# Later mixing of v, a new spread of conv taps, and output weights split in other steps, in a hybrid encoder layer on one core

## Chip, cores and metric

The kernel runs on 1 core of one Trainium2 chip. The metric is the time of the device for one execution, in microseconds (us). Five engines work side by side, each with its own queue of instructions: TensorE (PE, matmuls and transposes), VectorE (DVE), ScalarE (ACT), GpSimd (POOL) and SyncE (SP), which here issues every DMA.

## The reference

One layer of an encoder: x of 2048 tokens by 1024 is normalised, multiplied by one input matrix, and the columns go to three mixers, each with a gate. Their outputs are concatenated, multiplied by an output matrix, added to the normalised x and normalised again. Cut to what is computed:

```python
x = layer_norm(x, ln_in_g, ln_in_b)
h = einsum('bsd,de->bse', x, w_in)
au, av, ag, ba, bb, bg, cq, ck, cv, cg = split(h, ...)   # 256 x6, 512, 128, 128, 512
# A: spatial gating in chunks of 128 tokens, 4 heads of 64
v  = layer_norm(gelu(av), ln_g, ln_b)
v  = einsum('hij,bcjhd->bcihd', w_spatial, v) + b_spatial
ya = gelu(au) * v * silu(ag)
# B: depthwise convolution, 31 taps over the tokens, 256 channels
y  = conv(ba * sigmoid(bb), conv_w) + conv_b
yb = silu(layer_norm(y, g, b)) * silu(bg)
# C: attention over +-128 tokens, 8 query heads, 2 key/value heads, sink and bias
yc = attention(cq, ck, cv, sink, bias) * silu(cg)
y  = concatenate([ya, yb, yc]) @ w_out
out = layer_norm(2 ** 0.25 * x + y, post_ln_g, post_ln_b)
```

All arrays are float32.

## The kernel before

**Products.** Every product of the large matrices is made from two parts, a rounded `hi` and the rest `lo`: `hi*hi + hi*lo + lo*hi`, three matmuls. The normalised x lies transposed in four tiles `xc0` to `xc3` of 512 tokens, hi and lo. `feat(w, c, ...)` makes one tile `ft_n_c` of 128 columns by 512 tokens in 24 matmuls of 128x512 (lines 139 to 141). The weights of a column block come as `raw_f`, are rounded by ACT to `hi_f` and subtracted to `lo_f`.

**Stages.** First the layer norm of x, the columns av (written to DRAM as `gv_d`), keys and values. Then 72 steps in the list `steps`, each one `feat` and its evacuation: steps 0 to 15 the conv's bb and ba (n = 0 to 3), 16 to 31 the pairs au and ag (n = 4 to 7), 32 to 47 the queries (n = 8 to 11, evacuated to `qh_d` and `ql_d`), 48 to 55 cg (gates of the attention, silu, to `g_d`), 56 to 63 bg, and from `tail0` = 64 on the pairs (16, c), (17, c), that is the rest of cg, mixed with slots of the attention (`SLOTS`). Behind the steps the attention and the output projection run block by block of 128 tokens to the end.

**Work hung on the steps.** `hooks` holds functions for a step. `vln_tile(t)` loads a tile `gw` of gelu(av), normalises it on DVE (with two small operations on GpSimd, `nse` and `nsr`) and writes it hi and lo into `vacc`, `vglu` or, for the last four, `vshi`/`vslo`. `spatial(g)` mixes four such tiles: four tiles `sp` of PSUM (pool tag psE, two buffers, which `ft` tiles of odd steps use too), whose sum with the bias ACT copies to `so`, to be stored. `turn_spatial` transposes the spatial weights `wsr` through `ps_wt`; `prep_conv` loads and transposes the conv weights `cwr` through `ps_cw`. `cwr` and the `gw` tiles share the tag "cn" with two buffers. `conv_step(n)` emits n of the conv's 62 operations on DVE into `acc0`, then `acc1` (line 399); a sum `taps` decides how many a step gets, the last two come in step 47. From `cl0` = 48 on `conv_ln_tile` transposes `acc` to tiles `cl`, normalises them, and `conv_back` turns them back. `split_wo(k, hf)` loads a piece `wor` of the output weights, makes `woh` (ACT) and `wol` (DVE) and stores both; its buffers (tags ug, shi, slo, two each) are those of the evacuations' hi and lo.

**Tail.** `open_f32` and `open_f32r` open arenas in the place of `xc0` and `xc1`, `open_wo(0)` loads the first half of the split output weights, `wo0`, into the place of `xc2`, `open_wo(1)` into that of `xc3`. `start_block(i)` loads q of block i in two DMAs (`qh_d`, `ql_d`) and casts it; `scores` makes `s{i}_{h}` and `ptrans` the transposes `pt`; `oproj` multiplies into `out{i}_{hf}`.

**What sets the order.** A scheduler sorts each engine's instructions by its own estimate of when they are ready; the order in the code is only its input. So an edit in the first steps can move instructions of the last ones. SP issues its DMAs strictly in its order, so one that waits for data or for a buffer holds all behind it; in the trace a DMA also waits for the one eight issues ahead of it (that of `gw` at 144.67 us for `wsr`).

Of the kernel before, what the change touches and what calls it, by code (L numbers as in the profile page):

```python
# [55 lines left out]
def trunk_kernel(  # L56
# [77 lines left out]
    def feat(w, c, name, o=0, n=CH, tag="psD"):  # L134
        ps = psp.tile([P, n], F32, tag=tag, name="ft_" + name)
        hi, lo = w
        for k in range(NK):
            xh, xl = xc[c][:, 0, k, o:o + n], xc[c][:, 1, k, o:o + n]
            T.matmul(ps, hi[:, k, :], xh, start=(k == 0), stop=False)  # L139
            T.matmul(ps, hi[:, k, :], xl, start=False, stop=False)  # L140
            T.matmul(ps, lo[:, k, :], xh, start=False, stop=(k == NK - 1))  # L141
        return ps
# [159 lines left out]
    def want(n):  # L302
        if n < len(plan) and n not in wts:
            wts[n] = prep_w(plan[n][0], f"f{n}", V if 4 <= n < 14 else G)
# [12 lines left out]
    def prep_conv():  # L317
        cwr = pm.tile([KW, 256], F32, tag="cn", name="cwr")
        SY.dma_start(cwr, conv_w[0])
        for j, src in enumerate((conv_b, conv_ln_g, conv_ln_b)):  # L320
            SY.dma_start(cpar[:, j, :], src[0].rearrange("(a p) -> p a", p=P))
        ps = psp.tile([P, 2, KW + 1], F32, tag="psE", name="ps_cw")
        for a in range(2):
            T.transpose(ps[:, a, 0:KW], cwr[:, a * P:(a + 1) * P], ident[0:KW, 0:KW])
        V.tensor_copy(cw[:, :, 0:KW], ps[:, :, 0:KW])
# [11 lines left out]
    def prep_spatial():  # L337
        wsr = pm.tile([P, 4, P], F32, tag="tmp", name="wsr")
        SY.dma_start(wsr, w_spatial[0].rearrange("h i j -> i h j"))
        SY.dma_start(bsp, b_spatial[0].rearrange("h i -> i h"))  # L340
        SY.dma_start(vgb[:, 0, :], gmlp_ln_g[0].partition_broadcast(P))
        SY.dma_start(vgb[:, 1, :], gmlp_ln_b[0].partition_broadcast(P))
        return wsr

    def turn_spatial(wsr):
        ps = psp.tile([P, 4 * P], F32, tag="psE", name="ps_wt")
        for h in range(4):
            T.transpose(ps[:, h * P:(h + 1) * P], wsr[:, h, :], ident)
        S.copy(wth, ps)
        V.tensor_tensor(out=wtl, in0=ps, in1=f32(wth), op=ALU.subtract)  # L350
# [19 lines left out]
    def spatial(g):  # L370

        so = [pm.tile([P, 2, 256], F32, tag="tmp", name=f"so{g}_{j}") for j in range(2)]
        for h in range(4):
            ps = psp.tile([P, TPC, HD], F32, tag="psE", name=f"sp{g}_{h}")
            fs = slice(h * HD, (h + 1) * HD)
            cs = slice(h * P, (h + 1) * P)
            if g < 3:
                parts = [(ps, varena[g % 2][:, 0, :, fs], varena[g % 2][:, 1, :, fs])]
            else:
                parts = [(ps[:, 2 * j:2 * j + 2, :], vsp[j][0][:, :, fs], vsp[j][1][:, :, fs]) for j in range(2)]  # L380
            for o, vh, vl in parts:
                T.matmul(o, wth[:, cs], vh, start=True, stop=False)
                T.matmul(o, wth[:, cs], vl, start=False, stop=False)
                T.matmul(o, wtl[:, cs], vh, start=False, stop=True)
            for j in range(2):
                S.activation(so[j][:, :, fs], ps[:, 2 * j:2 * j + 2, :], AF.Identity, bias=bsp[:, h:h + 1])
        for j in range(2):
            r0 = (g * TPC + 2 * j) * P
            SY.dma_start(spo_d[r0:r0 + 2 * P, :].rearrange("(c p) f -> p c f", p=P), so[j])
# [17 lines left out]
    def conv_step(n):  # L407
        for _ in range(n):
            if avail[0] <= 0:
                return  # L410
            avail[0] -= 1
            next(conv)
# [42 lines left out]
    def load_mixed(a, c):  # L455
        sp = pm.tile([P, TPC, P], F32, tag="ug", name=f"spo{a}_{c}")
        SY.dma_start(sp, spo_d[c * CH:(c + 1) * CH, a * P:(a + 1) * P].rearrange("(b p) f -> p b f", p=P))
        spo[a, c] = sp

    def mixed(a, c):  # L460
        sp = spo.pop((a, c))
        pt = psp.tile([P, CH], F32, tag="psA", name=f"spT{a}_{c}")
        for j in range(TPC):
            T.transpose(pt[:, j * P:(j + 1) * P], sp[:, j, :], ident)
        spt[a, c] = pt
        u = a * NC + c + 1
        if u < 2 * NC:
            load_mixed(u // NC, u % NC)

    def evac(kind, a, c, ps):  # L470
        cs = slice(c * CH, (c + 1) * CH)
        ps_cs = slice(PAD + c * CH, PAD + (c + 1) * CH)
        if kind == "bb":
            if c == 0:
                g_ = pm.tile([P, SEQ + 2 * PAD + 2], F32, tag="glu", name=f"glu{a}")
                V.memset(g_[:, 0:PAD], 0.0)
                V.memset(g_[:, PAD + SEQ:SEQ + 2 * PAD], 0.0)
                glu.append(g_)
            S.activation(glu[a][:, ps_cs], ps, AF.Sigmoid)
        elif kind == "ba":  # L480
            last[0] = V.tensor_tensor(out=glu[a][:, ps_cs], in0=ps, in1=glu[a][:, ps_cs], op=ALU.mult).ins
            if c == NC - 1:
                avail[0] += KW
        elif kind == "au":
            tm = pm.tile([P, CH], F32, tag="tmp", name=f"gu{a}_{c}")
            S.activation(tm, ps, AF.Gelu_apprx_tanh)
            pt = spt.pop((a, c))
            last[0] = V.tensor_tensor(out=tm, in0=pt, in1=tm, op=ALU.mult).ins
            ug[a, c] = tm
        elif kind == "cq":  # L490
            fs = slice(a * P, (a + 1) * P)
            split_store(ps, qh_d[fs, cs], ql_d[fs, cs], -(HD ** -0.5), pm, 2)
        else:
            tm = pm.tile([P, CH], F32, tag="tmp", name=f"{kind}{a}_{c}")
            S.activation(tm, ps, AF.Silu)  # L495
            if kind == "ag":
                up = ug.pop((a, c))
                last[0] = V.tensor_tensor(out=up, in0=tm, in1=up, op=ALU.mult).ins
                store_y(a, c, up)
            elif kind == "bg":  # L500
                G.tensor_tensor(out=tm, in0=tm, in1=ybt[a][:, cs], op=ALU.mult)
                store_y(2 + a, c, tm)
            else:
                SY.dma_start(g_d[a * P:(a + 1) * P, cs], tm)
# [87 lines left out]
    def load_v(i):  # L592
        SY.dma_start(f32(ar["v"][i % 8]), v_d[i].rearrange("p a l d -> p a (l d)"))
# [219 lines left out]
    def at(s, fn, *args):  # L813
        hooks.setdefault(s, []).append((fn, args))
# [10 lines left out]
    for c in range(NC):  # L825
        steps += [(16, c), (17, c)]

    at(0, prep_conv)
    for t in range(NT):
        at(t // 2, vln_tile, t)  # L830
    cl0 = 48
    for t in range(NT):
        at(cl0 + t // 2, conv_ln_tile, t)
        at(cl0 + t // 2 + 1, conv_back, t)
    for j in range(16):
        at(32 + j, split_wo, j % 8, j // 8)
    wsr = prep_spatial()

    taps = 0.0
    for s, (n, c) in enumerate(steps):  # L840
        want(n)
        if c == 0:
            want(n + 1)
        if c == 1:
            want(n + 2)
        kind = plan[n][1]
        if s == 1:
            turn_spatial(wsr)
        if s in (4, 6, 8, 10):
            spatial(s // 2 - 2)  # L850
        if s == 13:
            load_mixed(0, 0)
        if kind == "au":
            mixed(plan[n][2], c)
        ps = feat(wts[n], c, f"{n}_{c}", tag="psE" if s > 11 and kind != "bg" and s % 2 else "psD")
        evac(kind, plan[n][2], c, ps)
        for fn, args in sorted(hooks.get(s, []), key=lambda e: e[0] is vln_tile or e[0] is conv_ln_tile):
            fn(*args)
        if s == cl0 - 1:
            conv_step(2 * KW)  # L860
        elif s >= 8:
            taps += 1.0 if s < 12 else 1.625
            if s < 12:
                conv_step(int(taps))
            else:
                with tc.issue_after(last[0]):
                    conv_step(int(taps))
            taps -= int(taps)
        r = s - tail0
        if r == 0:  # L870
            load_k()
        if r == 1:
            open_f32()
        if r == 3:
            open_f32r()
            load_v(0)
            load_v(1)
        if r == 5:
            open_wo(0)
        for h in range(SLOTS[max(r, 0)], SLOTS[max(r + 1, 0)]):  # L880
            slot(h // 8, h % 8)
# [40 lines left out]
```

## Time and profile before

| | us |
|---|---|
| median of 3 runs | 873.06 |
| the runs | 871.87, 873.63, 873.06 |
| the profiled execution | 874.27 |
| its span in the trace | 872.5 |
| PE busy in the span | 829.8 |
| DVE busy | 570.6 |
| ACT busy | 353.8 |
| POOL busy | 279.4 |

The profile is of one execution. Its span is the time from the first to the last instruction; 1.8 us of the execution lie around it. PE is busy for 95% of the span. A row of a timeline gives the start and the length in us, the engine, the line of the code, the operation, what it writes and reads, its size and how many such operations the row joins; in square brackets stands the idle time of the engine ahead of it and what ended that. "SPq" is the queue of SP; its rows show the issue of a DMA, not its transfer.

### The profile page before, as it was taken

What the parts mean: (1) busy time and instruction counts of PE and PEld (TensorE: products, weight loads), DVE (VectorE), ACT (ScalarE), POOL (GpSimd) and SP (SyncE); (2) the same over time, 40 slices, a digit from 0 to 9 for tenths busy, and PEclk for the clock granted to TensorE, in tenths of its full rate; (3) what the DMA queues carried; (4) which work ended last, traced back from release to release, by engine and by line L of the source; (5) the groups of instructions that cost most, each with busy time, mean ns of one, the idle gap of its engine ahead of it and who ended that gap; (6) DMA issues with size and microseconds to landing.
All of it is one profiled execution on the core that took longest, in us unless ns stands there. A gap on an engine that the chain in (4) does not pass through costs nothing.

```text
span 872.5 us, 12065 instructions
## 1 busy us (share of the span) xinstructions
PE 829.8 (95%) x4260; PEld 699.5 (80%) x4260; DVE 570.6 (65%) x1004; ACT 353.8 (41%) x764; POOL 279.4 (32%) x324
## 2 busy tenths in 40 slices
PE   4889998899999999999899999999899999999996
PEld 3889887677888888888788887788788888888875
DVE  5688612673578888999732111577678887777764
ACT  2654222332033433222122222874665565665540
POOL 4542111431000000000333311014566665566654
PEclk9999999999999999999999999999999999999999
DMA  7777524331022324877414568987654455442221
GB/s 231 242 254 258 190 85 111 103 108 43 25 73 73 121 73 170 281 251 264 167 61 99 179 202 192 275 325 183 155 143 116 115 142 155 115 117 90 85 84 62
DMA packets 115864, 131.23 MB, mean 150 GB/s; under 512 B 8692, under 2 KB 87059, under 8 KB 115260
## 3 DMA queue, kind: packets, MB, share of 16 engines
q1 hardware_dynamic: 115804, 130.47, 48.6%
q8 instruction: 33, 0.54, 0.3%
q14 instruction: 27, 0.22, 0.1%
HBM read 75.90 MB, written 55.07 MB: 150 GB/s over the span
## 4 chain that ended last, share of the span: by engine, by line
PE 63%; DVE 13%; POOL 8%; DMA 8%; issue 3%; ACT 3%; SPq 1%; POOLq 0%; DVEq 0%; ACTq 0%
PE ft L141 11%; PE ft L139 11%; PE ft L140 11%; PE out L720 3%; PE out L722 3%; PE out L721 3%; PE pt L675 3%; DVE acc L399 3%; POOL arena L667 2%; PE s L642 2%; PE pv L692 2%; PE pv L693 2%; POOL arena L707 2%; POOL nsr L107 2%; DMA x<-in_x_dram 1%
## 5 line engine op out<-in xcount | busy, mean ns | idle before, releaser
L139 PE MATMUL ft<-xc,hi_f 128*128 128x512 f32 x576 | 226.6, 393 | 0.0
L141 PE MATMUL ft<-xc,lo_f 128*128 128x512 f32 x576 | 225.0, 391 | 0.0
L140 PE MATMUL ft<-xc,hi_f 128*128 128x512 f32 x576 | 225.0, 391 | 0.0
L399 DVE SCALAR_TENSOR_TENSOR acc<-glu,cw,acc 128x2048 f32<-128x2048 f32 x60 | 140.7, 2345 | 0.4
L141 PEld LDWEIGHTS ft<-xc,lo_f 128*128 128x128 f32 x576 | 108.4, 188 | 22.6
L139 PEld LDWEIGHTS ft<-xc,hi_f 128*128 128x128 f32 x576 | 108.4, 188 | 22.1 <-DVE smg L645 0.2
L140 PEld LDWEIGHTS ft<-xc,hi_f 128*128 128x128 f32 x576 | 108.5, 188 | 21.7
L131 POOL TENSOR_TENSOR lo_f<-raw_f,hi_f 128x1024 fp32r<-128x1024 f32 x8 | 21.4, 2670 | 266.5 <-ACT hi_f L129 266.5
L658 ACT ACTIVATE arena<-arena,smg 128x288 f32<-128x288 f32 (+4 forms) x128 | 67.4, 527 | 56.8 <-DVE smg L645 55.7
L645 DVE CUSTOM_DVE_ANT_0 arena<-s,arena,nsink 128x288 f32<-128x288 f32 (+4 forms) x128 | 62.6, 492 | 37.4 <-DMA arena<-qh_d 19.3
L680 DVE TENSOR_TENSOR arena<-pt,arena 128x512 fp32r<-128x512 f32 x92 | 62.7, 684 | 15.2 <-ACT arena L679 15.0
L679 ACT CAST arena<-pt 128x512 fp32r<-128x512 f32 x92 | 53.2, 581 | 30.2 <-PE pt L675 29.7
L675 PE MATMUL pt<-ident,arena 128*128 128x128 f32 x368 | 55.9, 273 | 5.8 <-DVE arena L680 5.8
L705 POOL TENSOR_TENSOR arena<-arena,gt 128x512 f32<-128x512 f32 x16 | 20.7, 1292 | 119.0 <-DVE arena L698 85.8
L642 PEld LDWEIGHTS s<-k,q 128*128 128x128 f32 x256 | 46.7, 188 | 13.0 <-DVE smg L645 1.7
L642 PE MATMUL s<-k,q 128*128 128x288 f32 (+4 forms) x256 | 54.3, 296 | 1.3 <-ACT cg L495 0.7
L667 POOL TENSOR_SCALAR arena<-arena,sml 128x288 f32<-128x288 f32 (+2 forms) x104 | 50.4, 504 | 6.6 <-ACT bot L696 5.0
L675 PEld LDWEIGHTS pt<-ident,arena 128*128 128x128 f32 x368 | 43.9, 140 | 9.8 <-issue 4.6
L720 PE MATMUL out<-wo,yh 128*128 128x512 f32 x124 | 51.2, 413 | 0.0
L720 PE MATMUL out<-wo,arena 128*128 128x512 f32 x124 | 48.8, 394 | 0.0
L721 PE MATMUL out<-wo,yh 128*128 128x512 f32 x124 | 48.7, 392 | 0.0
L721 PE MATMUL out<-wo,arena 128*128 128x512 f32 x124 | 48.5, 391 | 0.0
(184 smaller groups left out, 1596.6 us busy)
## 6 DMA issues: line engine op xcount, KB each, us to landing
raw_f<-in_w_in_dram SPq DMA_DIRECT2D x18, 512.0 KB, 4.3
xhat_d<-x SPq DMA_DIRECT2D x16, 512.0 KB, 6.1
r<-xhat_d SPq DMA_DIRECT2D x16, 512.0 KB, 3.6
x<-in_x_dram SPq DMA_DIRECT2D x15, 512.0 KB, 4.9
out_dram<-r SPq DMA_DIRECT2D x15, 512.0 KB, 3.2
yh_d<-shi SPq DMA_DIRECT2D x16, 256.0 KB, 2.3
yl_d<-slo SPq DMA_DIRECT2D x16, 256.0 KB, 2.4
qh_d<-shi SPq DMA_DIRECT2D x16, 256.0 KB, 2.2
```

Source lines behind the costliest of these rows:

```text
L139: T.matmul(ps, hi[:, k, :], xh, start=(k == 0), stop=False)
L140: T.matmul(ps, hi[:, k, :], xl, start=False, stop=False)
L141: T.matmul(ps, lo[:, k, :], xh, start=False, stop=(k == NK - 1))
L399: V.scalar_tensor_tensor(out=acc[a], in0=glu[a][:, k:k + SEQ], scalar=cw[:, a, k:k + 1], in1=acc[a], op0=ALU.mult, op1=ALU.add)
L642: T.matmul(ps[:, 0:n], d["q"][:, h, :], kt[e * 2 + kv][:, g0:g0 + n], start=(e == 0), stop=(e == 1))
L645: V.tensor_tensor_reduce(out=s[:, k0:k1], in0=ps[:, 0:n], in1=ar["bias"][:, kv, b0:b0 + n], scale=1.0, scalar=nsink[:, h:h + 1], op0=ALU.a ...
L658: S.activation(p, p, AF.Exp, bias=d["g"][:, h:h + 1], scale=-1.0, accum_out=d["l"][:, h:h + 1])
L667: (V if i < 3 else G).tensor_scalar(out=p, in0=p, scalar1=d["l"][:, h:h + 1], scalar2=1.0, op0=ALU.mult, op1=ALU.mult)
L675: T.transpose(ps[:, r, :], d["p"][kv * 4 + r][:, f0:f0 + P], ident)
L680: V.tensor_tensor(out=pl, in0=pf, in1=f32(ph), op=ALU.subtract)
L720: T.matmul(ps, hi, wh, start=(k == 0), stop=False)
L721: T.matmul(ps, hi, wl, start=False, stop=False)
```

## The change

The hooks that feed the mixing of v move back by two steps: tiles 8 to 15 of `vln_tile` run in steps 6 to 9 instead of 4 to 7, `spatial(0)` to `spatial(3)` in steps 6, 8, 10, 12 instead of 4, 6, 8, 10, the first load of mixed v in step 14 instead of 13. `prep_conv` keeps the loads and is called ahead of the steps; the transposes become `turn_conv`, called in step 3. The taps are spread as 1.0 a step in steps 8 to 11 as before, then 1.7 up to step 31 and 1.5 in the queries' steps, in place of 1.625 throughout. `split_wo` runs in steps 48 to 63 instead of 32 to 47.

```diff
@@ -319,6 +319,9 @@
         SY.dma_start(cwr, conv_w[0])
         for j, src in enumerate((conv_b, conv_ln_g, conv_ln_b)):
             SY.dma_start(cpar[:, j, :], src[0].rearrange("(a p) -> p a", p=P))
+        return cwr
+
+    def turn_conv(cwr):
         ps = psp.tile([P, 2, KW + 1], F32, tag="psE", name="ps_cw")
         for a in range(2):
             T.transpose(ps[:, a, 0:KW], cwr[:, a * P:(a + 1) * P], ident[0:KW, 0:KW])
@@ -825,16 +828,16 @@
     for c in range(NC):
         steps += [(16, c), (17, c)]
 
-    at(0, prep_conv)
     for t in range(NT):
-        at(t // 2, vln_tile, t)
+        at(t // 2 + 2 * (t >= 8), vln_tile, t)
     cl0 = 48
     for t in range(NT):
         at(cl0 + t // 2, conv_ln_tile, t)
         at(cl0 + t // 2 + 1, conv_back, t)
     for j in range(16):
-        at(32 + j, split_wo, j % 8, j // 8)
+        at(48 + j, split_wo, j % 8, j // 8)
     wsr = prep_spatial()
+    cwr = prep_conv()
 
     taps = 0.0
     for s, (n, c) in enumerate(steps):
@@ -846,9 +849,11 @@
         kind = plan[n][1]
         if s == 1:
             turn_spatial(wsr)
-        if s in (4, 6, 8, 10):
-            spatial(s // 2 - 2)
-        if s == 13:
+        if s == 3:
+            turn_conv(cwr)
+        if s in (6, 8, 10, 12):
+            spatial(s // 2 - 3)
+        if s == 14:
             load_mixed(0, 0)
         if kind == "au":
             mixed(plan[n][2], c)
@@ -859,7 +864,7 @@
         if s == cl0 - 1:
             conv_step(2 * KW)
         elif s >= 8:
-            taps += 1.0 if s < 12 else 1.625
+            taps += 1.0 if s < 12 else 1.7 if s < 32 else 1.5
             if s < 12:
                 conv_step(int(taps))
             else:
```

**Where the instructions stand.** On PE near the start, in the second and third tile of the first weights (here `ft_1` and `ft_2`, in the words above `ft_0_1` and `ft_0_2`), before:

```order
L141 MATMUL ft_2_1556<-xc_98,lo_f_1388 128x512
L139 MATMUL ft_2_1556<-xc_98,hi_f_1386 128x512
L140 MATMUL ft_2_1556<-xc_98,hi_f_1386 128x512
L324 MATMUL ps_cw<-ident,cwr 128x31 x2
L348 MATMUL ps_wt<-ident,wsr 128x128 x4
L141 MATMUL ft_2_1556<-xc_98,lo_f_1388 128x512
```

and now, the transposes of the spatial weights in `ft_0_1`,

```order
L141 MATMUL ft_1_1498<-xc_97,lo_f_1388 128x512
L139 MATMUL ft_1_1498<-xc_97,hi_f_1386 128x512
L140 MATMUL ft_1_1498<-xc_97,hi_f_1386 128x512
L351 MATMUL ps_wt<-ident,wsr 128x128 x4
L141 MATMUL ft_1_1498<-xc_97,lo_f_1388 128x512
L139 MATMUL ft_1_1498<-xc_97,hi_f_1386 128x512
```

those of the conv weights between `ft_0_2` and `ft_0_3`:

```order
L140 MATMUL ft_2_1552<-xc_98,hi_f_1386 128x512
L141 MATMUL ft_2_1552<-xc_98,lo_f_1388 128x512
L327 MATMUL ps_cw<-ident,cwr 128x31 x2
L139 MATMUL ft_3_1610<-xc_99,hi_f_1386 128x512
L140 MATMUL ft_3_1610<-xc_99,hi_f_1386 128x512
```

`ps_wt` stands nine matmuls earlier than it did, `ps_cw` 19 later. The four groups of the mixing move in the same listing too: `sp0` from inside `ft_1_0` to behind `ft_1_1`, `sp1` from behind `ft_1_1` to behind `ft_1_3`, `sp2` from behind `ft_1_3` to behind `ft_2_1`, `sp3` from behind `ft_2_1`, in five pieces, to behind `ft_2_3`, in one piece.

On SP in the tail, around the loads of the first blocks of q. `g_d<-cg_1_4438` is the store of `cg3_1`, which comes from `ft_17_1`; `g_d<-cg_1_4410` that of `cg2_1`, from `ft_16_1`; the arenas are those opened in the place of `xc0` (4379) and `xc1` (4441); the first `qh_d` and `ql_d` load q0, the next q1. Before:

```order
L504 DMA g_d<-cg_0_4376 128x512
L551 DMA arena_4379<-rep_d 32x2x288 x3
L604 DMA arena_4379<-qh_d 64x8x128
L504 DMA g_d<-cg_1_4410 128x512
L605 DMA arena_4379<-ql_d 64x8x128
L604 DMA arena_4379<-qh_d 64x8x128
L605 DMA arena_4379<-ql_d 64x8x128
L593 DMA arena_4441<-v_d 128x256
L504 DMA g_d<-cg_1_4438 128x512
L593 DMA arena_4441<-v_d 128x256 x2
```

and now:

```order
L507 DMA g_d<-cg_0_4376 128x512
L554 DMA arena_4379<-rep_d 32x2x288 x4
L507 DMA g_d<-cg_1_4410 128x512
L507 DMA g_d<-cg_1_4438 128x512
L596 DMA arena_4441<-v_d 128x256 x2
L607 DMA arena_4379<-qh_d 64x8x128
L608 DMA arena_4379<-ql_d 64x8x128
L607 DMA arena_4379<-qh_d 64x8x128
L608 DMA arena_4379<-ql_d 64x8x128
```

Both stores of gates and two loads of `v_d` have come ahead of the loads of q0.

On PE in the tail, behind the last scores of block 0, before:

```order
L642 MATMUL s_7_4520<-k_4342,q_4446 128x256
L642 MATMUL s_7_4520<-k_4348,q_4446 128x256
L675 MATMUL pt_0_1_4569<-ident,arena_4379 128x128 x2
L139 MATMUL ft_2_4576<-xc_98,hi_f_4205 128x512
L140 MATMUL ft_2_4576<-xc_98,hi_f_4205 128x512
L141 MATMUL ft_2_4576<-xc_98,lo_f_4207 128x512
```

and now:

```order
L678 MATMUL pt_0_1_4569<-ident,arena_4379 128x128
L645 MATMUL s_7_4520<-k_4342,q_4446 128x256
L645 MATMUL s_7_4520<-k_4348,q_4446 128x256
L678 MATMUL pt_0_1_4569<-ident,arena_4379 128x128 x2
L723 MATMUL out_0_4751<-wo_4604,yh_4545 128x512
L645 MATMUL s_0_4554<-k_4339,q_4538 128x288
L645 MATMUL s_0_4554<-k_4345,q_4538 128x288
```

`ft_2_4576` is `ft_17_2`, whose 24 matmuls stand ahead of `s0_0` now, where only one of them stood there; `s_0_4554` is `s1_0`, and `out_0_4751` is the first tile of the output projection, `out0_0`, whose first matmul has moved ahead of `s1_0` from behind `ft_16_3`.

## Rows read from the trace of the kernel before

**Rows 1.** Page, busy us (share of the span) by engine.
```profile
PE 829.8 (95%) x4260; PEld 699.5 (80%) x4260; DVE 570.6 (65%) x1004; ACT 353.8 (41%) x764; POOL 279.4 (32%) x324
```

**Rows 2.** Timeline of PE: start, us, engine, line, operation, [idle before, releaser].
```profile
147.06 0.28 PE L324 MATMUL ps_cw<-ident,cwr 31*128 31x31 f32 x2 [2.37 <-DMA cwr<-in_conv_w_dram]
...
159.27 0.51 PE L382 MATMUL sp<-vacc,sparena 128*128 128x256 f32 x2 [0.21 <-ACT vacc L367]
...
190.41 0.38 PE L382 MATMUL sp<-vacc,sparena 128*128 128x256 f32 x1 [1.95 <-ACT so L386]
...
204.57 0.44 PE L382 MATMUL sp<-vshi,sparena 128*128 128x128 f32 x2 [1.19 <-ACT vshi L367]
```

**Rows 3.** Timeline of DVE, then of PE, around the last tap.
```profile
424.30 2.34 DVE L399 SCALAR_TENSOR_TENSOR acc<-glu,cw,acc 128x2048 f32<-128x2048 f32 x1
...
426.70 0.55 PE L420 MATMUL cl<-ident,acc 128*128 128x128 f32 x3 [2.58 <-DVE acc L399]
```

**Rows 4.** Timeline of ACT, then of PE, in the attention's fifth block.
```profile
612.46 0.62 ACT L608 CAST q<-arena 128x512 fp32r<-128x512 f32 x1 [4.94 <-DMA arena<-ql_d]
...
614.98 0.66 PE L675 MATMUL pt<-ident,arena 128*128 128x128 f32 x4 [2.86 <-DVE arena L680]
```

**Rows 5.** Stretches: length, busy PE, PEld, DVE, ACT, POOL; PEclk, DMA share, GB/s.
```profile
125.00:225.00 100.00, 92.07 (x419) 74.01 (x418) 46.88 (x103) 28.90 (x69) 26.49 (x35) 0.98 0.32 96
207.00:210.40 3.40, 3.40 (x13) 2.94 (x12) 0.00 (x0) 1.25 (x4) 0.00 (x0) 0.50 0.21 71
400.00:425.00 25.00, 24.11 (x107) 19.66 (x106) 24.96 (x19) 6.20 (x10) 4.33 (x1) 1.00 0.67 238
425.00:450.00 25.00, 23.30 (x117) 19.58 (x117) 8.88 (x24) 4.08 (x6) 7.87 (x17) 1.00 0.23 75
525.00:550.00 25.00, 23.83 (x114) 19.20 (x113) 5.05 (x24) 10.40 (x23) 3.95 (x1) 1.00 0.91 198
```

**Rows 6.** Timelines of PE and SP; SP's waits (total, times, longest us).
```profile
132.03 0.39 PE L139 MATMUL ft<-xc,hi_f 128*128 128x512 f32 x1
132.25 0.39 PE L140 MATMUL ft<-xc,hi_f 128*128 128x512 f32 x1
...
144.67 0.34 SPq L356 DMA_DIRECT2D gw<-gv_d  x1
...
SPq L356 <- DMA wsr<-in_w_spatial_dram: 0.3, 1, 0.3
```

**Rows 7.** Timeline of ACT ahead of the copies of sp2.
```profile
188.79 1.04 ACT L129 CAST hi_f<-raw_f 128x1024 fp32r<-128x1024 f32 x1
```

**Rows 8.** Timelines of ACT, SP and PE where block 0 starts.
```profile
537.13 1.14 ACT L608 CAST q<-arena 128x512 fp32r<-128x512 f32 x2 [4.42 <-DMA arena<-ql_d]
...
537.50 0.35 SPq L593 DMA_DIRECT2D arena<-v_d  x1
538.79 0.33 SPq L504 DMA_DIRECT2D g_d<-cg  x1
539.17 1.14 SPq L593 DMA_DIRECT2D arena<-v_d  x2
...
537.80 0.69 PE L642 MATMUL s<-k,q 128*128 128x160 f32 x4
```

**Rows 9.** DMA: issues, KB each, median us to landing; 532 to 546, then 554 to 556.
```profile
arena<-ql_d SPq DMA_DIRECT2D x3, 256.0 KB, 4.6
...
yl<-yl_d SPq DMA_DIRECT2D x2, 256.0 KB, 6.6
...
wo<-woh_d SPq DMA_DIRECT2D x1, 512.0 KB, 4.5
```

**Rows 10.** Timeline of PE, first and last row around the transposes of block 0.
```profile
545.86 0.37 PE L642 MATMUL s<-k,q 128*128 128x192 f32 x2
...
548.52 0.48 PE L139 MATMUL ft<-xc,hi_f 128*128 128x512 f32 x1
```

**Rows 11.** Timeline of GpSimd in the norm of v.
```profile
200.61 2.20 POOL L105 TENSOR_SCALAR nse<-nsm 128x1 f32<-128x1 f32 x1 [5.75 <-DVE nsm L116]
```

## The prediction

> **What bounds the kernel now.** I read the page's table of busy time first: TensorE (PE) is busy 829.8 of 872.5 us [rows 1], so what a change of order can win or lose lies in the 42.7 us without work. Then PE's timeline: every row with idle time ahead of it, and the releaser named there; then the rows of the queue or engine that the releaser lives on. Three places lie in what the change touches. (a) Early, PE waits 2.37 for the conv weights and then five times, 5.35 together, for the mixing of v, first at 159.27 (.21) and last at 204.57 (1.19); the longest is 1.95 [rows 2]. (b) Behind the last tap, which starts at 424.30 and takes 2.34, PE waits 2.58 for the transposes of `acc` [rows 3]. (c) In the attention, 2.86 at 614.98 [rows 4]. A table by stretches gives the weight of (a): PE is busy 92.07 of the 100 us from 125 to 225 [rows 5]. Nothing else that DVE, ACT and GpSimd do in these stretches is waited for.
>
> What a gap costs: a 128x512 matmul is shown .39 long, but the next starts .23 behind it [rows 6], so a gap costs its idle time and .16 more. The five gaps of the mixing are worth 5.35 + .80 = 6.15 us, that of the conv weights 2.53, the tap's 2.74.
>
> **The change, part by part.** *Turning of the weights.* `ps_cw` moves behind `ft_0_2`, where its data are long there: 2.53 us go. But `ps_wt` now stands behind 20 of the 24 matmuls of `ft_0_1`, so 44 matmuls and four transposes behind 132.03 [rows 6]: at about 142.5. It reads `wsr`, and the queue's load of `gw` at 144.67 is held for the end of `wsr`'s by its last .3 us [rows 6], so that `wsr` lands at 144.6. A new wait of 2.1 (1.9 to 2.4) takes the old one's place: net -0.4.
>
> *Mixing of v.* All four groups go two steps back in PE's order, 9.5 to 11 us each. Against that, `cwr` holds one of two "cn" buffers until `ps_cw`, so the second `gw` load and the LN chain behind it start some 4.5 us later than now. sp1 and sp2 keep several us of lead. At sp0, ACT's order has a `vglu` cast, which waits for that chain, ahead of the copies that free sp0's buffers: 1.3 (0 to 3). At sp3 it has a `hi_f` cast of 1.04 [rows 7] ahead of them, and there are two psE buffers: 1.0 (0 to 2). 6.15 go, 2.3 come, and sp3 in one piece for five spares about .5 of switching between tiles: net -4.3. Behind the last of the five gaps PE was granted .50 of its clock, 1.2 GHz, for 3.40 us [rows 5]: 1.7 lost. The gaps of 2.37, 2.58 and 2.86 were followed by no such stretch. I count it neither way and put 1.7 on both sides.
>
> *Taps.* 4 + 20 x 1.7 + 15 x 1.5 = 60.5 against 4 + 35 x 1.625 = 60.9: both have 60 of 62 done by step 46. What changes is what shares DVE's time in the query steps: 1.5 x 2.34 = 3.5 us of taps for 3.8, and no `wol`. DVE was busy 24.96 of 25 in the last of them [rows 5]; it will have time to spare, and the last two taps start without a backlog. In PE's order the transposes of acc0 now stand behind the last query tile and those of acc1 two matmuls into the next. The 2.74 go. Before the queries 1.7 taps (4.0 of 5.44 us a step) and the products with the gates fill DVE to about 92%; a backlog under a step is not seen by PE: 0.
>
> *Split of the output weights.* 24 loads, 16 casts on ACT, 16 subtractions on DVE and 32 stores leave steps 32 to 47 for 48 to 63. What hides them: DVE is busy 8.88 of 25 us behind 425, with DMA at .23; the query steps bore all of this beside as many stores of their own, with DMA at .67 [rows 5]. SP issues in order, so a load that waits for a buffer holds the stores behind it; their first reader is `wo0`, step 69. 0, and -1 to +1 as bounds for the places that it takes from `cl` and the weights' `lo_f`.
>
> *Tail.* The scheduler's order changed here too, though no line of it did. (i) `q0`'s loads stood ahead of the store of `cg3_1`, and q0 was cast at 537.13, .67 ahead of its first use [rows 8]. Now that store and two `v_d` stand ahead of them. `ft_17_1` ended at 537.5, the store was issued at 538.79, two `v_d` at 539.17 take 1.14; `qh0` would follow at 540.3 and `ql0` at 541.0, 3.5 behind the end of `ft_17_1`. Such loads land in 4.6 [rows 9], half of the cast takes .57: 8.6. PE has the 24 matmuls of `ft_17_2`, 5.45. A new wait of 3.1 (2.6 to 4). (ii) The first matmul of `out0_0` stood behind all of `ft_17_2` and `ft_16_3`. Now it stands behind `s0_7` and the last transposes of `pt0_0_1`, whose piece took from 545.86 to 548.52, 2.66 [rows 10]. Its `wo0` takes over the buffer of `xc2`, whose last reader, now `ft_16_2`, ends just ahead of that piece; .2 to issue and 4.5 to land [rows 9] make 4.7. A new wait of 2.1 (1 to 4). (iii) At 614.98 it was ACT that was late: its copy of q5 had waited 4.94 for a load [rows 4] and held what the transposes need. It now stands three operations later: 1.0 (0.5 to 2) goes.
>
> Sum: -0.4 - 4.3 - 2.7 + 0 + 3.1 + 2.1 - 1.0 = -3.2. The profiled execution took 874.27, so 871.1 by it; the median of the three runs is 1.2 lower, 873.06, which gives 869.9.
>
> A row that speaks against moving LN work: a GpSimd operation on one element a partition, `nse`, took 2.20 at 200.61, in the time of a tap [rows 11]. The Trainium skill, "SBUF — State Buffer", section "Who interferes with whom", states that a VectorE instruction with two SBUF inputs contends with a GpSimd one that reads SBUF. The trace agrees; by that rule LN work two steps later would meet more taps and be up to two us a tile later, as in R3 below. What speaks against it here is DVE's own order: the last three tiles' LN now stands ahead of the first tap, where it was mixed with taps before.
>
> **Rivals.** R1, *the tail's loads are covered*: the two new waits don't come, since ACT or the order of issues gives the 3.1 and 2.1 elsewhere. For it: PE hardly waited between 525 and 560. Against: the releases are read from rows. The gains alone are -8.4: 864.7. R2, *the tail's loads are longer than I take*: they share SP's queue, with DMA .91 busy from 525 to 550 [rows 5], and `yl` took 6.6 there [rows 9]. With 2 to 2.5 us more on each the waits are 5.5 and 4.5, and if each is followed by 3.40 us at 1.2 GHz, twice 1.7: +13.4 against -8.4, slower, 878.1. It decides where the tail costs over 8.4. R3, *v's chain is late again*: the loads behind `cwr` put `vacc` and `vshi` where PE waits for them as now, the 4.3 don't come: 874.2, no difference.
>
> The Trainium skill, "TensorE: Matmul & The Clock Gate", section "What's actually happening", states that the slow clock is the default and activity lifts it; by that each new gap could bring such a stretch. The trace shows it behind one of the four gaps named.
>
> **How the numbers follow.** Forecast 0.55 (869.9, its own range 867 to 873), R1 0.17, R2 0.14, R3 0.14. 0.2% is 1.75 us, about what a measurement of this kernel can tell from no change: 871.3 to 874.8. Faster: R1, 0.41 of the forecast's 0.55, and 0.03 of R3: 0.61. Within: 0.12 of the forecast, 0.10 of R3: 0.22. Slower: R2, 0.02 of the forecast, 0.01 of R3: 0.17. Eight in ten reach from somewhat under R1 to above R3: 863.8 to 875.5.
>
> **What would show it.** Right: no wait at `ps_cw`, one of 2 at `ps_wt` with `wsr` as its releaser; PE over 95 of 100 us busy from 125 to 225; no wait at `cl`; a wait of 3 at `s0_0` whose end is q's cast; one of 2 at `out0_0`, released by the load of `wo`; under 2 in the place of the 2.86. Wrong: `vacc` or `vshi` as releaser of over 2 us at sp0 or sp3 (R3); the 2.58 still there (DVE fuller than I count); no wait at `s0_0` (R1). A time under 866 means that the tail gave nothing back, over 875 that it took more than the start gained.

## The result: slower by 0.6%

The changed kernel took 878.61 us (median of 10 runs, 876.20 to 881.89) against 873.35 for the kernel before (10 runs, 871.16 to 876.48): ratio 1.0062, 95% interval 1.0042 to 1.0082, or +5.4 us. The forecast was 869.9, its range 863.8 to 875.5. The profiled execution of the changed kernel took 876.20, span 874.4, and is the fastest of its ten; what sets it apart from the median is told below.

### The profile page after: what moved, and what is told of

Read it like the earlier page. It is cut to its first block, busy times and chain, and to the rows that moved or that the text cites. A ratio compares the mean times of both kernels' runs of the same rounds, so it can differ in the third digit from the quotient of the medians.

```text
span 874.4 us, 12070 instructions
## 1 busy us (share of the span) xinstructions
PE 830.4 (95%) x4260; PEld 700.8 (80%) x4260; DVE 573.6 (66%) x1004; ACT 353.7 (40%) x764; POOL 276.9 (32%) x324
## 4 chain that ended last, share of the span: by engine, by line
PE 65%; DVE 11%; POOL 9%; DMA 5%; ACT 5%; issue 3%; SPq 1%; POOLq 0%; DVEq 0%; ACTq 0%
PE ft L139 12%; PE ft L140 12%; PE ft L141 12%; PE out L725 3%; PE out L723 3%; PE out L724 3%; POOL arena L670 3%; PE pt L678 2%; DMA arena<-ql_d 2%; PE s L645 2%; POOL arena L710 2%; POOL nsr L107 2%; PE pv L695 2%; PE pv L696 2%; PE xT L207 1%
```

## The profile after

PE's waits come first, as before: the timeline of PE, start, length, line, operation, and in brackets the idle time ahead and its releaser.

```profile
142.78 0.63 PE L351 MATMUL ps_wt<-ident,wsr 128*128 128x128 f32 x4 [1.82 <-DMA wsr<-in_w_spatial_dram]
...
169.86 0.38 PE L385 MATMUL sp<-vacc,sparena 128*128 128x256 f32 x1 [2.11 <-ACT so L389]
...
196.69 0.38 PE L385 MATMUL sp<-vacc,sparena 128*128 128x256 f32 x1 [1.31 <-ACT so L389]
...
210.03 0.33 PE L385 MATMUL sp<-vshi,sparena 128*128 128x128 f32 x1 [0.68 <-ACT so L389]
...
418.86 0.44 PE L423 MATMUL cl<-ident,acc 128*128 128x128 f32 x2 [1.29 <-DVE acc L402]
...
537.31 2.90 PE L645 MATMUL s<-k,q 128*128 128x160 f32 x9 [2.64 <-ACT q L611]
...
551.60 0.50 PE L723 MATMUL out<-wo,yh 128*128 128x512 f32 x1 [0.97 <-DMA wo<-woh_d]
553.33 0.80 PE L645 MATMUL s<-k,q 128*128 128x288 f32 x4 [1.23 <-ACT q L611]
...
592.98 0.50 PE L724 MATMUL out<-wo,arena 128*128 128x512 f32 x1 [1.28 <-DMA wo<-wol_d]
...
620.03 0.63 PE L678 MATMUL pt<-ident,arena 128*128 128x128 f32 x4 [1.77 <-POOL r L762]
```

The first four rows answer [rows 2]: no wait for the conv weights, one for `wsr`, and three waits in the mixing, all for copies to `so`, where there were five, four of them for `vacc`, `vglu` and `vshi`. The fifth answers [rows 3], the last [rows 4]. The waits at 537, 551, 553 and 593 are new. What stands behind the one at 537, in the timelines of SP and ACT (these answer [rows 8]):

```profile
530.37 0.87 SPq L596 DMA_DIRECT2D arena<-v_d  x2
531.29 0.63 SPq L607 DMA_DIRECT2D arena<-qh_d  x1
531.97 0.63 SPq L608 DMA_DIRECT2D arena<-ql_d  x1
...
536.64 1.14 ACT L611 CAST q<-arena 128x512 fp32r<-128x512 f32 x2 [6.73 <-DMA arena<-ql_d]
```

`ql0` is issued at 531.97, 1.6 us behind the first of two loads of `v_d`, which themselves stand behind the store of `cg3_1`; ACT has it 4.67 later.

The wait at 553, of s1_0, is not for a late load. The second half of q1 was issued at 533.32 and landed in 6.2; ACT casts q1 at 552.68 without idle time ahead of it, at the end of a chain of its own work that starts with the gate of `ft_16_2`:

```profile
549.26 0.60 ACT L498 ACTIVATE cg<-ft 128x512 f32<-128x512 f32 x1
549.87 1.28 ACT L661 ACT_TABLE_LOAD   x1
...
552.68 1.12 ACT L611 CAST q<-arena 128x512 fp32r<-128x512 f32 x2
```

The rows left out are exponentials of block 0. s1_0 starts 4.07 behind that `cg`. In the kernel before, 13 matmuls of `ft_16_3`, from 548.52 to 551.60, stood ahead of s1_0 on PE and covered this chain; now `ft_16_3` starts at 560.20. So the waits at 551 and 553, .97 and 1.23, are with the .50 of out0_0's matmul between them one gap of 2.70, and ACT ends it.

Then stretches (length, busy PE, PEld, DVE, ACT, POOL, granted clock of PE, DMA share, GB/s); the first four stand beside [rows 5], the last three show the clock behind the new waits:

```profile
125.00:225.00 100.00, 94.08 (x443) 77.39 (x442) 51.54 (x105) 28.46 (x69) 24.19 (x35) 1.00 0.31 92
400.00:425.00 25.00, 23.71 (x110) 19.22 (x109) 19.34 (x18) 5.19 (x9) 5.75 (x5) 1.00 0.44 155
425.00:450.00 25.00, 25.00 (x127) 20.96 (x126) 11.73 (x30) 8.77 (x15) 8.27 (x17) 1.00 0.70 243
525.00:550.00 25.00, 21.38 (x88) 16.99 (x86) 4.54 (x21) 7.45 (x18) 0.00 (x0) 0.86 0.83 191
...
537.50:544.50 7.00, 6.72 (x20) 5.34 (x20) 3.66 (x17) 3.98 (x13) 0.00 (x0) 0.51 1.15 256
544.50:554.00 9.50, 6.61 (x34) 4.92 (x33) 2.67 (x13) 5.99 (x13) 0.00 (x0) 1.00 0.86 218
554.50:558.50 4.00, 4.00 (x16) 3.31 (x17) 3.29 (x11) 3.94 (x6) 0.00 (x0) 0.57 0.83 278
```

From s0_0 on PE ran 7 us at 1.2 GHz, and behind the wait at 553 some 3.4 us more; the two cost 7.00 x .49 = 3.4 and 4.00 x .43 = 1.7. In the kernel before the clock was full through this whole part.

The ledger, worked out from the starts of the same instructions on PE in both timelines (us):

| part of PE's work | before | after | difference |
|---|---|---|---|
| start of the span to `ft_0_0` | 132.03 | 130.33 | -1.70 |
| to the first transposes of mixed v (`spT`) | 108.35 | 102.92 | -5.43 |
| to the last of these | 79.61 | 79.61 | 0 |
| to the first `cb` (conv_back) | 112.57 | 111.30 | -1.27 |
| to the last block's output tile (`outl`) | 426.54 | 436.90 | +10.36 |
| to PE's last matmul | 5.91 | 5.91 | 0 |

The first row holds nothing of the change: before has a stretch at 1.2 GHz at 46.5 to 50.0, after one at 29.0 to 32.5, and the rest varies between executions. The second holds the 1.7 of the stretch in [rows 5] that after didn't have. So what the early part gained was lost, and more, in the tail, and 5.1 of the tail's 10.4 is clock.

## The experiments

Medians of ten runs (seven of split_alone, four of late_q0), and ratio to the kernel before run on the same chip:

| kernel | us | ratio | 95% interval |
|---|---|---|---|
| changed | 878.61 | 1.0062 | 1.0042 to 1.0082 |
| mix_alone | 869.84 | 0.9962 | 0.9939 to 0.9986 |
| taps_alone | 874.00 | 1.0027 | 1.0010 to 1.0045 |
| split_alone | 880.19 | 1.0077 | 1.0050 to 1.0104 |
| no_split | 869.59 | 0.9979 | 0.9960 to 0.9997 |
| late_q0 | 883.47 | 1.0113 | 1.0063 to 1.0163 |
| split_44 | 869.35 | 0.9967 | 0.9942 to 0.9993 |
| early_q0 | 872.82 | 1.0011 | 0.9992 to 1.0030 |
| early_q0_late_out | 869.42 | 0.9984 | 0.9968 to 1.0000 |
| fill22 | 874.50 | 1.0041 | 1.0013 to 1.0068 |
| turn_3 | 868.64 | 0.9963 | 0.9944 to 0.9983 |
| sp0_first | 868.15 | 0.9980 | 0.9953 to 1.0007 |

**Which part loses.** The theory from the two traces: the early part gains, the split alone moves the order of the tail, and the order costs 10.

*mix_alone* keeps the change of hooks and takes back the other two:

```diff
-            taps += 1.0 if s < 12 else 1.7 if s < 32 else 1.5
+            taps += 1.0 if s < 12 else 1.625
-        at(48 + j, split_wo, j % 8, j // 8)
+        at(32 + j, split_wo, j % 8, j // 8)
```

> The mixing of v and the turning of the conv weights two steps on, alone; taps 1.625 a step and the split in steps 32 to 47 as before. Theory T (the early part gains what was forecast, and the tail's loss comes from the split alone, through the order of SP and PE): the tail has the order of before, so no wait of 2.6 at s0_0; the mixing reaches the gates of au about 7 us earlier, as in the changed kernel, and keeps it: 873.3 - 6 to - 8 = 865.3 to 867.3, with the wait at cl still there. Rival U (the loss comes from the early part itself, work two steps later that has to be made up in the tail): 876 to 879.

Measured: 869.84, ratio 0.9962. Faster, but by half of what was expected. In its trace the way to the first `spT` is 102.94, as in the changed kernel, the tail 425.99, as before. PE's timeline has the wait at cl of before and none at s0_0 for q:

```profile
172.34 0.38 PE L385 MATMUL sp<-vacc,sparena 128*128 128x256 f32 x1 [2.10 <-ACT so L389]
...
199.05 0.38 PE L385 MATMUL sp<-vacc,sparena 128*128 128x256 f32 x1 [1.20 <-ACT so L389]
...
422.00 0.55 PE L423 MATMUL cl<-ident,acc 128*128 128x128 f32 x3 [2.63 <-DVE acc L402]
...
534.17 0.85 PE L645 MATMUL s<-k,q 128*128 128x224 f32 x4 [0.35 <-DVE smg L648]
```

*split_alone* is the kernel before with the one line of the split:

```diff
-        at(32 + j, split_wo, j % 8, j // 8)
+        at(48 + j, split_wo, j % 8, j // 8)
```

> The split of the output weights in steps 48 to 63 alone; mixing and taps as before. T: the early waits are those of before, the wait at cl goes or shrinks (-1.5 to -2.7), the tail has the changed order: waits of 2.6 at s0_0, 1.0 at out0_0, 1.2 at s1_0 and stretches at 1.2 GHz behind them, together +10: 880 to 882, the slowest of this group. U: 870.5 to 872, the wait at cl gone and nothing else.

Measured: 880.19, ratio 1.0077. The wait at cl, 2.58 in the kernel before and 1.29 in the changed one, is gone altogether, so it is the split that frees DVE there. The tail's four waits are there:

```profile
543.38 0.69 PE L642 MATMUL s<-k,q 128*128 128x160 f32 x4 [2.87 <-ACT q L608]
...
556.66 0.50 PE L720 MATMUL out<-wo,yh 128*128 128x512 f32 x1 [1.18 <-DMA wo<-woh_d]
...
558.18 1.29 PE L642 MATMUL s<-k,q 128*128 128x288 f32 x4 [1.02 <-ACT q L608]
...
596.80 0.50 PE L721 MATMUL out<-wo,arena 128*128 128x512 f32 x1 [0.82 <-DMA wo<-wol_d]
```

*taps_alone* is the kernel before with the line of the taps:

```diff
-            taps += 1.0 if s < 12 else 1.625
+            taps += 1.0 if s < 12 else 1.7 if s < 32 else 1.5
```

> 1.7 taps a step up to the queries and 1.5 in them, alone. T: the wait at cl (2.6 before) falls to between 1 and 2.5, since DVE has one tap less in eight steps but the wol still beside it; nothing else moves: 870.5 to 872.5, not to be told from the kernel before with 872.2. Rival: the shift of taps frees DVE as forecast and the wait goes: 869.5.

Measured: 874.00, ratio 1.0027, a little slower than before, which neither expected. The wait at cl is 2.16 for 2.58, so the shift of taps without that of the split takes 0.4 from it. In this execution a stretch at 1.2 GHz followed the wait at cl and another the one of 2.77 in the attention; over its ten runs span x (1 - granted clock) is 8.4 us in the mean, 5.2 for the kernel before beside it. So the loss is in the clock, but why more such stretches come in this kernel is open.

*no_split* is the changed kernel with the split in steps 32 to 47:

```diff
-        at(48 + j, split_wo, j % 8, j // 8)
+        at(32 + j, split_wo, j % 8, j // 8)
```

> The changed kernel with the split of the output weights left in steps 32 to 47, so mixing and taps alone. Theory T (the order of the tail comes from the split alone): the tail as before, no wait over 1 between 530 and 560, no stretch at half clock there; the early part as in the changed kernel, the wait at cl between 1 and 2.7: 867 to 870, as the run with the mixing alone (869.8) or up to 1.5 better for the taps.

Measured: 869.59, ratio 0.9979. Together: the mixing alone is worth about -3, the taps nothing or a small loss, and the split by itself +7, its gain at cl included.

**Order or traffic?** The split brings 24 loads and 32 stores to the steps ahead of the tail, and it brings another order to SP. *late_q0* takes the order without the traffic: in the kernel before, one edge.

```diff
+                gst[a, c] = SY.dma_start(g_d[a * P:(a + 1) * P, cs], tm).ins
...
+        with tc.issue_after(gst[3, 1]):
             SY.dma_start(raw[0:HD], qh_d.rearrange("(h d) t -> d h t", d=HD)[:, :, cs])
             SY.dma_start(raw[HD:P], ql_d.rearrange("(h d) t -> d h t", d=HD)[:, :, cs])
```

> The kernel before with one edge in SP's order: the two loads of q0 are issued behind the store of cg3_1. Nothing is added or left out, the split stays in steps 32 to 47. T (the order is the cause, not the 24 loads and 32 stores that the split brings to steps 48 to 63): the wait of 2.6 at s0_0 and the stretch at half clock behind it appear here too, and PE's order of the tail follows: +8 to +10, 881 to 883. Rival D (the moved DMAs make the tail's loads slow): the wait is at most 1, +0 to +2, 873 to 875.

Measured: 883.47, ratio 1.0113. PE's order followed the edge, with all of `ft_17_2` ahead of s0_0 and out0_0 ahead of s1_0, and the waits came:

```profile
544.36 0.86 PE L643 MATMUL s<-k,q 128*128 128x160 f32 x4 [2.42 <-ACT q L609]
...
559.15 0.47 PE L721 MATMUL out<-wo,yh 128*128 128x512 f32 x1 [1.44 <-DMA wo<-woh_d]
560.41 0.80 PE L643 MATMUL s<-k,q 128*128 128x288 f32 x4 [0.79 <-ACT q L609]
...
563.84 0.79 PE L722 MATMUL out<-wo,yh 128*128 128x512 f32 x1 [1.17 <-DVE smg L646]
```

*split_44* takes the traffic, nearly all of it, without the order:

```diff
-        at(48 + j, split_wo, j % 8, j // 8)
+        at(44 + j, split_wo, j % 8, j // 8)
```

> The changed kernel with the split in steps 44 to 59 in place of 48 to 63. In its order the loads of q0 stand ahead of the store of cg3_1 again and out0_0 behind ft_16_3. T: the early gain of 7 is kept, the wait at cl is at most 2.7, no wait over 1 at s0_0 and out0_0, PE at full clock from 530 to 560: 864 to 867. D: 12 of 16 pieces still lie in steps 48 to 59, so most of the loss stays: 874 to 878.

Measured: 869.35, ratio 0.9967, faster than both kernels. So it is the order: twelve of the sixteen pieces still lie in steps 48 to 59, and nothing of the loss is left. The 869.35 are above the 864 to 867 expected, by the early part (below).

*early_q0* mends the order in the changed kernel, with two edges, the loads traced one step earlier:

```diff
+            elif (a, c) == (3, 1):
+                with tc.issue_after(q0[0]):
+                    SY.dma_start(g_d[a * P:(a + 1) * P, cs], tm)
...
+        if r == 2:
+            start_block(0)
         if r == 3:
             open_f32r()
-            load_v(0)
-            load_v(1)
+            with tc.issue_after(q0[0]):
+                load_v(0)
+                load_v(1)
```

(`q0[0]` is the load of `ql0`.)

> The changed kernel with two edges in SP's order: the two loads of q0 are traced one step earlier, and the store of cg3_1 and the first two loads of v are issued behind them. Nothing is added or left out. T: the wait of 2.6 at s0_0 goes and with it the two stretches of half clock behind it (3.4); out0_0 moves behind s1_1, so its wait and that at s1_0 shrink by about 1: 878.6 - 2.8 - 3.4 - 1 = 871 to 874. Rival D (all transfers of the tail are late because of the moved DMAs): the wait only moves to s1_0 or out0_0, 876 to 879.

Measured: 872.82, ratio 1.0011. The wait at s0_0 is gone, but ahead of s1_0 stands one of 2.69, for ACT's cast of q1, where the changed kernel had .97, a matmul of .50 and 1.23; and three for `wo`, .48 to 1.21, came at 585 to 592, where it had one of 1.28. So taking out0_0 away left that gap as long as it was. In this kernel, the changed one, split_alone and fill22 (below) s1_0 starts 4.07 behind the `cg` of `ft_16_2` on ACT, in late_q0 4.06. *early_q0_late_out* also holds out0_0 back on PE:

```diff
+            with tc.issue_after(st[1]["sc"]):
                 oproj(0, 0, h)
```

(`st[1]["sc"]` is the last matmul of block 1's scores.)

> As early_q0, and in addition out0_0's matmuls stand behind the last scores of block 1 on PE, by an edge. T: no wait over 1 at s0_0, out0_0 and s1_0, full clock from 530 to 560; what the early part gained is kept: 868 to 870, as with the split in steps 44 to 59 (869.3). Rival D: 874 to 878, waits at the loads of q1 or wo.

Measured: 869.42, ratio 0.9984. The wait for q1 (2.70, 4.06 behind that `cg`) is still there, against the expectation, with two slow stretches from 547.5 on: `ft_16_3` still stands behind s1_0. Those for `wo` are gone, and so is most of the loss. No run moved `ft_16_3` alone; split_44, where 13 of its matmuls stand ahead of s1_0 again, has no wait there.

**What the clock adds.** The stretch 525 to 575 in five kernels, each its own row, in this order: before, changed, split_alone, late_q0, split_44. The last but two numbers are the granted clock.

```profile
525.00:575.00 50.00, 48.81 (x239) 39.92 (x238) 21.26 (x74) 32.00 (x71) 6.61 (x3) 1.00 0.88 235
...
525.00:575.00 50.00, 43.96 (x194) 35.27 (x193) 20.69 (x73) 29.18 (x67) 2.66 (x2) 0.90 0.84 237
...
525.00:575.00 50.00, 43.76 (x199) 35.44 (x198) 16.89 (x64) 26.02 (x57) 4.48 (x2) 0.93 0.86 237
...
525.00:575.00 50.00, 42.97 (x177) 34.27 (x176) 14.04 (x54) 22.08 (x51) 3.95 (x1) 0.86 0.74 202
...
525.00:575.00 50.00, 48.80 (x244) 40.14 (x243) 22.93 (x80) 34.34 (x76) 5.37 (x3) 1.00 0.88 249
```

Each of the kernels in which PE waited at s0_0, out0_0 and s1_0 has lost clock here, and none of those in which it didn't. Does the idle time do that? *fill22* leaves the order of the changed kernel and lets PE work through the wait:

```diff
+        if (i, h) == (0, 0):
+            with tc.issue_after(lastmm[0]):
+                for _ in range(22):
+                    T.matmul(ps, wts[17][0][:, 0, :], xc[3][:, 0, 0, 0:WK], start=True, stop=True)
```

(`lastmm[0]` is the last matmul of `ft_17_2`; `ps` is the tile of s0_0.)

> The changed kernel, in whose order PE waits at s0_0 for q0, with 22 more matmuls of 128x288 on PE between ft_17_2 and s0_0, into the tile of s0_0, which s0_0 then overwrites; they read what lies there anyway. ft_17_2 is traced earlier so that they can be placed, its place on PE is unchanged. They are extra work of about 2.6 us in the time of the wait of 2.64. Theory C (the half clock behind s0_0 comes from PE's idle time): no stretch at 1.2 GHz between s0_0 and out0_0, where the changed kernel had 7 us of it; one or none behind out0_0; 878.6 - 3.4 = 875.2, 874 to 876.5. Rival E (the stretch comes with the start of the attention, whatever PE did ahead of it): 878 to 880, the stretch stays, or the extra matmuls push s0_0 later.

Measured: 874.50, ratio 1.0041. PE's timeline, then the stretch from the first scores to the end of `ft_16_2`:

```profile
534.43 3.06 PE L649 MATMUL s<-xc,hi_f 128*128 128x288 f32 x22
537.32 0.64 PE L651 MATMUL s<-k,q 128*128 128x160 f32 x4
...
550.30 0.50 PE L729 MATMUL out<-wo,yh 128*128 128x512 f32 x1 [2.04 <-DMA wo<-woh_d]
...
537.30:545.30 8.00, 7.40 (x36) 5.98 (x35) 3.51 (x17) 4.14 (x13) 0.00 (x0) 1.00 1.14 261
```

s0_0 starts where it did (537.32 for 537.31), since it waits for the same load, but the clock is 1.00 behind it where it was .51. Over ten runs span x (1 - clock) is 6.4 us in the mean, 10.4 for the changed kernel, while the rest of the span is equal (866.1 and 866.4). So the idle time brings the slow stretch. The kernel with 22 matmuls of no use is the faster one by 1.8 us by the two ratios, whose intervals overlap, and by 4.1 by the two medians (whose runs of before stand 2.1 apart); the stretch cost 3.4. The next wait, at out0_0, was still followed by one (552.0 to 555.5).

**The early part.** *turn_3* takes split_44 and moves the turning of the spatial weights:

```diff
-        if s == 1:
+        if s == 3:
             turn_spatial(wsr)
```

> The split in steps 44 to 59, and the turning of the spatial weights moved from step 1 to step 3, behind ft_0_2, where their load has landed; else as split_44. Theory: the wait of 1.5 to 2.1 for wsr at ps_wt goes with its .16 and the stretches at half clock that follow it in some executions, nothing else moves: 869.3 - 1.8 to - 2.8 = 866.5 to 867.5, faster than both kernels. Rival: the chain of LN behind ps_wt's copies (wth, wtl on ACT and DVE) shifts by as much, and the wait at sp0 grows by what is gained: 869.

Measured: 868.64, ratio 0.9963. The wait for `wsr` is gone and PE waits as much longer at sp0. *sp0_first* then puts the casts of LN tiles 6 and 7 behind the copies of sp0 on ACT:

```diff
-        at(t // 2 + 2 * (t >= 8), vln_tile, t)
+        at(6 if t in (6, 7) else t // 2 + 2 * (t >= 8), vln_tile, t)
...
+        if t in (6, 7):
+            with tc.issue_after(so_last[0]):
+                S.copy(vh, gv)
+        else:
+            S.copy(vh, gv)
```

(`so_last[0]` is the last copy of sp0.)

> As turn_3, and on ACT the casts of the LN tiles 6 and 7 stand behind the copies of sp0 by an edge, their functions being traced in step 6. Nothing is left out. Theory (PE's wait at sp0 is ACT waiting, in its order, for the cast of tile 6, which the LN chain has ready 2.2 us behind that of tile 5): the wait of 4.07 falls to 1.9, the cast of tile 6 follows the copies; 868.6 - 2.2 and a stretch at half clock less in some executions: 865 to 866.5. Rival: the chain slips as much at sp1 and sp2, whose waits grow, and the time stays at 868.6.

Measured: 868.15, ratio 0.9980. The rows of turn_3 and of sp0_first:

```profile
169.15 0.58 PE L385 MATMUL sp<-vacc,sparena 128*128 128x256 f32 x1 [4.07 <-ACT so L389]
...
165.77 0.38 PE L391 MATMUL sp<-vacc,sparena 128*128 128x256 f32 x1 [1.64 <-ACT so L395]
...
195.46 0.58 PE L391 MATMUL sp<-vacc,sparena 128*128 128x256 f32 x1 [3.72 <-ACT so L395]
```

1.64 at sp0 as expected, and 3.72 at sp2: both rivals were right. Moving an order within the mixing moves the waits, since the chain of LN, two to four us a tile on DVE, GpSimd and one ACT queue, is what runs late.

## Why the prediction was wrong

The sum had a term too few, the clock behind the new waits, and two that were too large; and one wait of the tail had another cause than the one named.

*Early part: forecast -4.7, measured -3.0.* `ps_wt` waits 1.82 (2.1), sp0 2.11 (1.3), sp3 0.68 (1.0), and the releasers are those named: ACT stands at a `vglu` cast that waits for the LN chain (168.88, 1.81 idle), and the copies follow at 169.19. Not seen was sp2 with 1.31, and PE was busy 94.08 of the 100 us for which over 95 was the sign. In the seven profiled executions whose mixing is shifted as in the change, the way from `ft_0_0` to the first `spT`, less 1.7 for each stretch at half clock in it, is 102.6 in the mean; in the four with the old mixing, before among them, it is 105.6. So "net -4.3" was mis-sized: the five waits of 6.15 became three worth 4.10 + .48, not 2.3.

*Taps and cl: forecast -2.7, measured -1.3.* DVE did get its time back: in the 25 us up to the end of the last tap it is busy 21.18 us, where it was 24.91 (the row from 400 to 425 above reaches 6 us past that tap). By split_alone and taps_alone, without a wait here and with one of 2.16, this came from the split more than from the taps. But a wait of 1.29 stayed, and DVE's and GpSimd's timelines show another cause than a backlog:

```profile
407.27 7.12 DVE L402 SCALAR_TENSOR_TENSOR acc<-glu,cw,acc 128x2048 f32<-128x2048 f32 x3
...
414.91 3.89 DVE L402 SCALAR_TENSOR_TENSOR acc<-glu,cw,acc 128x2048 f32<-128x2048 f32 x1
...
412.38 4.27 POOL L131 TENSOR_TENSOR lo_f<-raw_f,hi_f 128x1024 fp32r<-128x1024 f32 x1 [212.94 <-ACT hi_f L129]
```

The last tap took 3.89 in place of 2.34 [rows 3], beside GpSimd's subtraction, which runs until 416.65; these 1.55 are more than the wait. The rule of the Trainium skill, "SBUF — State Buffer", section "Who interferes with whom", which the prediction set against the LN work, bore here instead: both instructions read two operands in SBUF. The trace agrees, and shows them one behind the other: the subtraction, 2.40 long at 438.10, ends 2.26 behind the three taps that end at 414.39, and the last tap ends 2.15 behind the subtraction. The kernel before had this too, which the prediction did not see in its 2.58; there the subtraction met a `wol` ahead of the last tap, .68 long elsewhere:

```profile
422.09 2.29 DVE L575 TENSOR_TENSOR wol<-wor,woh 128x512 fp32r<-128x512 f32 x1
...
419.50 4.33 POOL L131 TENSOR_TENSOR lo_f<-raw_f,hi_f 128x1024 fp32r<-128x1024 f32 x1 [215.94 <-ACT hi_f L129]
```

*Split: forecast 0.* Right in steps 48 to 63 themselves: PE is busy all of 100 us from 425 to 525.

*Tail, waits: forecast +4.2, measured +5.2* (10.36 less 5.1 of clock). s0_0 waited 2.64 (3.1); its place and cause were right, also that the order had changed without a line of the tail. out0_0 waited .97 (2.1) for the load named, but that load is not what PE lost time to: without out0_0 there the gap was 2.69 (early_q0). What opened it, as the rows read, is the move of `ft_16_3` behind s1_0, by which ACT's chain up to the cast of q1 came to lie open; the prediction did not ask for it, and the 1.23 at s1_0 stood in no term. So the forecast of 2.1 for a gap of 2.20 without work was luck. The wait of [rows 4] is 1.77 where it was 2.86 (-1.0 forecast), but split_alone and fill22, with the same split, have 2.39 and 2.37, early_q0 none over .3, and six kernels with the split elsewhere 2.02 to 2.77, so that the order did this is not shown. Unlisted was also 1.28 at 593, for a load of the second half of the output weights, the last of which was issued at 580.38, 2.46 later than before.

*Tail, clock: forecast 0, measured +5.1.* This is the step that failed: "I count it neither way", said of the stretch in [rows 5], and no such stretch put behind the new waits in the sum, only in R2. In the tail of the profiled execution there are stretches worth three times 1.7; in the ten runs span x (1 - clock) is 10.4 in the mean, against 5.2 to 6.6 for the kernel before in the groups here, +4 to +5. That also separates the profiled execution (clock .991) from the typical one (.988): .003 of 877 us is 2.6, and 878.6 - 876.2 is 2.4. I had four gaps with one stretch behind them and took that for a chance too small to count; with the two new waits of the forecast alone the same share would have asked for .9, and the rows of R2, with both, for 3.4.

With these, the last three from one execution, the sum is -3.0 - 1.3 + 5.2 + 5.1 = +6.0, against +5.4 measured. R2 named the right mechanism, waits and then half clock, and its 878.1 lies beside the 878.6 measured, but by another sum: it had longer waits than came, fewer slow stretches and larger gains. It got 0.14. Its condition, loads two us longer, did not come true: `ql0` landed in 4.6 as forecast, and PE had the first load of `wo0` 3.67 behind its issue at 547.93. The number of waits and the clock decided.

What stays open: why the scheduler's order flips between a split that starts in step 44 and one in 48, what `ft_16_3` alone would give back, and why `taps_alone` has more slow stretches.

## What to carry to other kernels

A wait of PE costs its length plus the half clock that it may bring; price both, here up to 1.7 for each of one or two stretches behind a wait of 1 to 3 us. Compare the order of all queues from end to end after an edit to a scheduled kernel, the tail too, and ask of each engine that ends a wait whether it was itself waiting: at s0_0 ACT stood for a load, at s1_0 it had worked without a pause since the gate of `ft_16_2`. A test of one edge in the order tells more than a test of the edit: late_q0 cost by itself about what the split did (1.0113 and 1.0077, intervals overlapping), and split_44 kept the gain.

## What the runs showed of the hardware

The slow stretches read here, the two ends of the span left out, last 3.4 us at .50 of the clock, worth 1.71 us, or twice that, and lie in or behind idle time of PE. Waits of the same length were followed by one in some executions and not in others (1.98 for `wsr` in mix_alone without, 2.07 in split_44 with one at 145.5 to 149.5). Much of the spread of the runs is this: the changed kernel ran from 876.20 at a clock of .991 to 881.89 at .985, .006 of 880 us being 5.3 of those 5.7, and that of mix_alone from 865.58 at .998 to 870.94 at .995, .003 being 2.6 of those 5.4.

The Trainium skill, "TensorE: Matmul & The Clock Gate", section "What's actually happening", says that activity lifts the clock from its slow default. fill22 agrees: matmuls of no use during the wait kept 1.00 where it had been .51.
